# Which queue issues the small transfers of a hybrid decoder layer: SyncE or GpSimd

## The chip, the cores and the metric

The kernel runs on one core of a Trainium2 chip. The metric is the device time of one execution in microseconds (us). The core's engines are TensorE (PE, with PEld for its weight loads), VectorE (DVE), ScalarE (ACT), GpSimd (POOL) and SyncE (SP); SP runs no arithmetic and here only issues transfers (DMAs). Each engine works through its own instructions in order and waits for others by semaphores.

## The reference

One layer of a decoder on 1024 tokens with 1024 features, all in float32. Two mixers read one common input projection:

```python
h = rmsnorm(x, norm1_w); proj = h @ w_in
o_a = gated_delta_rule(q_a, k_a, v_a, g, beta)              # 4 heads of 128, chunked
o_a = rmsnorm(o_a, gdn_norm_w) * silu(z)
o_b = dilated_attention(q_b, k_b, v_b)                      # 8 heads of 64, three (window, dilation) branches
x = x + concat([o_a, o_b]) @ w_out
h = rmsnorm(x, norm2_w)
u = causal_dwconv(h @ w_up, ffn_conv_w)                     # width 3
x = x + (silu(gate) * up) @ w_down
return rmsnorm(x, final_norm_w)
```

In the attention the three branches are merged by their softmax denominators; each output is a sum of values divided by one total denominator per token and head.

## The kernel before

Activations are kept with features on the 128 partitions and tokens along the row. Every large product is made of three TensorE products of split operands (`whi`, `wlo` and so on: a rounded high part and the rest). A weight tile is loaded into `wst` by SP, ScalarE rounds it into `whi`, and VectorE or, for the later dense tiles, GpSimd subtracts to give `wlo`.

A planner (`Weave`, line 49) runs generators for the parts of the layer (dense projections, the four heads' chains, attention, output projection, MLP) and chooses by estimated ready times which of them emits its next instructions. It fixes TensorE's order by a token on each product. The order on the other engines is then made by a scheduler that simulates the program, so that an instruction can be emitted earlier or later than its neighbours in the code. Objects of the class `Engine` hold the planner's costs and the engine that gets the instruction: `ve` and `uv` are VectorE, `ac` and `ua` ScalarE, `po_` GpSimd, `sy` transfers on SP, and `sq` small transfers, on SP too. Nearly all instructions carry line 142 or 144 (the helper in `Engine`), so they are told apart by their tiles.

`sq` is used in four places:

- `finish(h)` (line 926), for heads 2 and 3: the chain's output `vtok`, scaled on GpSimd by `ms`, is transposed in 32x32 blocks by VectorE into `ot`, and eight transfers per head write it to `odram` in runs of 32 numbers (512 runs each).
- `dense()` (line 617): four transfers per head read it back as `og` in 256 runs each. `og` is needed much later, when the gate `z` is multiplied in.
- `rows_out` (line 1052), for each of the attention's groups 0 to 6 (a group is half the tokens of one pair of heads): VectorE transposes the reciprocal denominators `dn` into `dt`, four transfers store it to `ddram`, two load it back as `rT`, each row repeated over 64 partitions.
- `rms2_power` (line 1291), once: the second norm's factors go through `ndram`; their broadcast load back into `rstdB` is issued by `sy`.

```python
    dt = tile_(sp, [P, 32], F32, "dt", "dt", 2)                                   # rows_out
    ve.transpose(dt, dns[g["n"] % 2])
    for b in range(4):
        sq.dma_start(to[:, 32 * b:32 * b + 32], dt[32 * b:32 * b + 8, :])
    rT = g["rT"] = tile_(sp, [P, 512], F32, "rT", "t2", 2)
    for e, er in enumerate(HALVES):
        sq.dma_start(rT[er].rearrange("p (u t) -> p u t", u=4), ...)
```

Attention is a pipeline over pairs of 128-row blocks; two pairs make a group. In each step (`advance`, line 1117) TensorE makes scores, VectorE adds the mask and takes the maximum (`sm`, `mx`), ScalarE exponentiates `sm`, TensorE transposes it, VectorE and ScalarE copy it to `pt` and `pb`, and TensorE multiplies with the values. `give` (line 1101) scales a finished group on VectorE: `oT` = sums times `rT`. Dense products (for `aqkv`, the next heads' queries and keys, drained by VectorE) fill TensorE between the steps. The tiles `ot`, `rT` and `oT` take turns in two buffers (`t2`). After the second norm's statistics, the first channel tile of the MLP is scaled as `xu` by `rstdB`, while VectorE goes on preparing weight blocks (`pair` and others).

Of the kernel before, what the change touches and what calls it, by code (L numbers as in the profile page):

```python
# [147 lines left out]
def hybrid_layer(tc, I, out):  # L148
    nc = tc.nc
    wv = Weave()  # L150
# [4 lines left out]
    ua = Engine(wv, nc.scalar, "scalar", 0.12, 0.00085, first=tc.high_priority)  # L155
    po_ = Engine(wv, nc.gpsimd, "gpsimd", 0.15, 0.0021)
    sy = Engine(wv, nc.sync, "sync", 0.05, 0.00142, 2.2)
    sq = Engine(wv, nc.sync, "small", 0.05, 0.00036, 0.4)
    sa = Engine(wv, nc.scalar, "actq", 0.05, 0.00142, 2.2)
    es = ExitStack()  # L160
    cp = es.enter_context(tc.tile_pool(name="cp", bufs=1))
# [1582 lines left out]
```

## Time and profile before

| | us |
|---|---|
| median of 3 runs | 1196.23 (1195.36 to 1197.35) |
| the profiled execution | 1197.55 |
| its span, first to last instruction | 1195.7 |
| TensorE busy | 1182.3 |
| VectorE / ScalarE / GpSimd busy | 918.3 / 569.5 / 81.5 |

The granted TensorE clock was 0.998 of full speed. Times in views are from the start of the span. SP's issues are shown with the time that the issue takes on SP, not with the transfer's flight. Nearly all transfers are on SP's queue.

### The profile page before, as it was taken

How to read it: one execution, taken by the hardware profiler on the slowest of the kernel's cores; microseconds unless marked ns; L12 is line 12 of the kernel's file. 1: busy time of each engine (PE TensorE's matmuls, PEld its weight loads, DVE VectorE, ACT ScalarE, POOL GpSimd, SP SyncE). 2: the span in 40 equal slices, each digit the busy share in tenths (PEclk: the TensorE clock that was granted, in tenths of full speed). 3: DMA queues.
4: the chain of work that ended last, by engine and by line, in shares of the span. 5: the costliest groups of instructions: out<-in, count | busy, mean ns of one | idle time of the engine just before them, and what ended most of it. 6: DMA issues, size and time to landing. Idle time of an engine off the chain costs nothing.

```text
span 1195.7 us, 18260 instructions
## 1 busy us (share of the span) xinstructions
PE 1182.3 (99%) x6998; PEld 977.3 (82%) x6998; DVE 918.3 (77%) x1473; ACT 569.5 (48%) x1115; POOL 81.5 (7%) x74
## 2 busy tenths in 40 slices
PE   9999999999999999999999999999999999999997
PEld 7888888888777778888888888888888888887886
DVE  7673975666365665777898898989889889998875
ACT  7275345355354533555554444445444453434441
POOL 0212010214211110000000000000000000000000
PEclk9999999999999999999999999999999999999999
DMA  7334234435944214443322313132231397546514
GB/s 244 101 95 150 80 116 127 143 122 172 220 147 129 86 52 135 159 159 106 106 86 73 106 53 106 54 106 81 78 103 56 127 368 284 197 160 211 168 53 141
DMA packets 100023, 157.20 MB, mean 131 GB/s; under 512 B 30400, under 2 KB 51168, under 8 KB 99936
## 3 DMA queue, kind: packets, MB, share of 16 engines
q1 hardware_dynamic: 99072, 155.25, 40.1%
q8 instruction: 55, 0.90, 0.3%
q10 hardware_dynamic: 864, 0.79, 0.2%
q14 instruction: 32, 0.26, 0.1%
HBM read 120.04 MB, written 35.96 MB: 130 GB/s over the span
## 4 chain that ended last, share of the span: by engine, by line
PE 93%; DVE 3%; ACT 2%; issue 1%; DMA 1%; POOLq 0%; POOL 0%; DVEq 0%; SPq 0%; ACTq 0%
PE ps L194 45%; PE pa L194 20%; PE dw L194 15%; PE pc L194 10%; PE ps L198 2%; DVE kT L142 1%; DMA wd<-in_wd 1%; DVE x1h L142 0%; ACT sm L144 0%; DVE pr L142 0%; DMA xt<-in_xT 0%; ACT whi L142 0%; DVE zz L142 0%; DVE wd L142 0%; ACT dec L142 0%
## 5 line engine op out<-in xcount | busy, mean ns | idle before, releaser
L194 PE MATMUL dw<-pr 128*128 128x512 f32 (+1 forms) x984 | 212.0, 377 | 0.3 <-DVE x1h L142 0.2
L194 PEld LDWEIGHTS dw<-pr 128*128 128x128 f32 x984 | 176.6, 188 | 34.7 <-DVE x1h L142 1.2
L194 PE MATMUL ps<-xhi,whi 128*128 128x512 f32 x384 | 157.1, 409 | 0.1
L194 PE MATMUL ps<-xhi,wlo 128*128 128x512 f32 x384 | 150.1, 391 | 0.0
L194 PE MATMUL ps<-xlo,whi 128*128 128x512 f32 x384 | 148.3, 390 | 0.0
L194 PE MATMUL pa<-T,pair 128*128 128x512 f32 x528 | 127.1, 389 | 0.1
L194 PEld LDWEIGHTS pa<-T,pair 128*128 128x128 f32 x528 | 99.0, 188 | 20.9 <-ACT u L142 0.5
L194 PEld LDWEIGHTS ps<-xhi,whi 128*128 128x128 f32 x384 | 72.3, 188 | 19.1 <-issue 5.6
L194 PEld LDWEIGHTS ps<-xhi,wlo 128*128 128x128 f32 x384 | 72.2, 188 | 15.6
L194 PEld LDWEIGHTS ps<-xlo,whi 128*128 128x128 f32 x384 | 72.3, 188 | 12.6
L142 ACT ACTIVATE u<-pa 128x512 f32<-128x512 f32 x44 | 26.3, 598 | 108.7 <-PE pa L194 108.7
L142 DVE SCALAR_TENSOR_TENSOR y<-xu,fcw,y 128x1023 f32<-128x1023 f32 (+1 forms) x44 | 56.4, 1281 | 23.3 <-ACT y L142 23.2
L142 ACT ACTIVATE whi<-wst 128x1024 fp32r<-128x1024 f32 x36 | 38.2, 1065 | 63.6 <-PE ps L194 45.9
L194 PE MATMUL pa<-B,A 128*128 128x512 f32 x264 | 63.4, 389 | 0.0
L194 PE MATMUL pc<-T,S 128*128 128x512 f32 x264 | 63.4, 389 | 0.0
L194 PE MATMUL pa<-T,S 128*128 128x512 f32 x264 | 63.4, 389 | 0.0
L194 PE MATMUL pc<-B,pair 128*128 128x512 f32 x264 | 63.4, 389 | 0.0
L142 ACT ACTIVATE pr<-r 128x1024 fp32r<-128x1024 f32 (+1 forms) x44 | 36.6, 840 | 51.8 <-PE dw L194 29.5
L142 DVE TENSOR_TENSOR wst<-wst 128x512 f32<-128x512 f32 x88 | 60.4, 687 | 0.8
L194 PE MATMUL ps<-B,pair 128*128 128x512 f32 x252 | 60.5, 389 | 0.0
L194 PEld LDWEIGHTS pa<-T,S 128*128 128x128 f32 x264 | 49.6, 188 | 10.3
L194 PEld LDWEIGHTS pc<-B,pair 128*128 128x128 f32 x264 | 49.6, 188 | 10.3
(255 smaller groups left out, 2322.5 us busy)
## 6 DMA issues: line engine op xcount, KB each, us to landing
wst<-in_wu SPq DMA_DIRECT2D x44, 512.0 KB
wd<-in_wd SPq DMA_DIRECT2D x44, 512.0 KB
upark<-y SPq DMA_DIRECT2D x22, 512.0 KB
wst<-in_wi SPq DMA_DIRECT2D x21, 512.0 KB
r<-upark SPq DMA_DIRECT2D x11, 512.0 KB
r<-upark SPq DMA_DIRECT2D x22, 256.0 KB
wa<-in_wd SPq DMA_DIRECT2D x22, 256.0 KB
wst<-in_wv SPq DMA_DIRECT2D x8, 512.0 KB
```

The lines of the kernel that those rows point to most:

```text
L142: return getattr(eng, op)(*a, **kw)
L194: tc.stamp_issue_order_token(nc.tensor.matmul(dst, lhs, rhs, start=start, stop=stop, **kw).ins, TOKEN)
L198: tc.stamp_issue_order_token(nc.tensor.transpose(dst, src, ident if idt is None else idt).ins, TOKEN)
```

## The change

The one object `sq` gets GpSimd in the place of SP. All its transfers (16 `odram`, 8 `og`, 28 `ddram`, 14 `rT`, 4 `ndram`) are issued by GpSimd then; the planner's costs for them stay.

```diff
     po_ = Engine(wv, nc.gpsimd, "gpsimd", 0.15, 0.0021)
     sy = Engine(wv, nc.sync, "sync", 0.05, 0.00142, 2.2)
-    sq = Engine(wv, nc.sync, "small", 0.05, 0.00036, 0.4)
+    sq = Engine(wv, nc.gpsimd, "small", 0.05, 0.00036, 0.4)
     sa = Engine(wv, nc.scalar, "actq", 0.05, 0.00142, 2.2)
```

TensorE's order is the same instruction for instruction. The scheduler places some others anew. GpSimd around the end of the chains and the first groups of attention, before (`vtok` and `ms` are a head's output and its factors, `wlo` a weight split, `pb` a cleared part of an attention tile):

```order
L142 TENSOR_TENSOR wlo<-wst,whi 128x1024
L142 MEMSET pb 32x2x128
L142 TENSOR_TENSOR ms<-ms,mhalf 128x8
L142 TENSOR_TENSOR vtok<-vtok,ms 128x1024
L142 TENSOR_TENSOR wlo<-wst,whi 128x1024 x2
L142 MEMSET pb 32x2x128
```

The same place in the changed kernel:

```order
L142 DMA odram<-ot 32x16x32 x8
L142 MEMSET pb 32x2x128
L142 TENSOR_TENSOR ms<-ms,mhalf 128x8
L142 TENSOR_TENSOR wlo<-wst,whi 128x1024
L142 DMA og<-odram 32x8x128 x4
L142 TENSOR_TENSOR vtok<-vtok,ms 128x1024
L142 DMA odram<-ot 32x16x32 x4
L142 TENSOR_TENSOR wlo<-wst,whi 128x1024
L142 DMA odram<-ot 32x16x32 x4
L142 DMA ddram<-dt 8x32 x4
L142 DMA og<-odram 32x8x128 x4
L142 DMA rT<-ddram 64x4x128 x2
```

Head 2's stores stand ahead of head 3's factors `ms`; head 2's loads `og`, which wait for those stores to land, stand ahead of head 3's scaling `vtok`; and group 0's `ddram` and `rT` stand behind head 3's stores and loads. For group 1 a `wlo` follows between `ddram` and `rT`; the same holds for groups 3 and 6.

VectorE at the start of attention, where head 3's output is transposed into `ot`, before:

```order
L142 TENSOR_SCALAR ms<-ms 128x8
L142 TENSOR_TENSOR aqkv<-ps,rstdB 128x4x32x4
L142 STREAM_TRANSPOSE ot<-vtok 128x128 x8
L142 TENSOR_TENSOR aqkv<-ps,rstdB 128x4x32x4
L144 ISA sm,mx<-ps,mk 128x128
```

And in the changed kernel:

```order
L144 ISA sm,mx<-ps,mk 128x256
L144 ISA mx 128x1
L144 RECIPROCAL dn<-mx 128x2
L142 STREAM_TRANSPOSE ot<-vtok 128x128 x8
L142 TENSOR_TENSOR aqkv<-ps,rstdB 128x4x32x4
L144 RECIPROCAL dn<-mx 128x2
```

The transposes of head 3 have moved behind the four `sm` and the first `dn` of the attention's first pair. They also wait now for head 2's stores, since both use the buffers of `ot`.

VectorE at the end of group 0, where `oT` of group 0 stands, before:

```order
L144 COPY pt<-ps 128x4x64
L144 COPY pb<-ps 128x2x64
L142 TENSOR_TENSOR oT<-ps,rT 128x4x4x32
L144 ISA sm,mx<-ps,mk 128x416
L144 ISA mx 128x1
```

And in the changed kernel:

```order
L144 ISA sm,mx<-ps,mk 128x448
L144 ISA mx 128x1
L144 RECIPROCAL dn<-mx 128x2
L142 TENSOR_TENSOR oT<-ps,rT 128x4x4x32
L144 RECIPROCAL dn<-mx 128x2
L142 STREAM_TRANSPOSE dt<-dn 128x32
L142 TENSOR_TENSOR aqkv<-ps,rstdB 128x4x32x4
```

`oT` of group 0 has moved behind the four `sm` of the next pair and one `dn`; `dt` of group 1 follows it. In groups 1 to 6 `oT` stands where it stood, ahead of the next pair's `sm`. In the first channel tile of the MLP, `xu` has moved behind one `pair` on VectorE.

## The prediction

> **What bounds the kernel now.** The page first: the busy times, then the chain that ended last.
>
> ```profile
> span 1195.7 us, 18260 instructions
> PE 1182.3 (99%) x6998; PEld 977.3 (82%) x6998; DVE 918.3 (77%) x1473; ACT 569.5 (48%) x1115; POOL 81.5 (7%) x74
> PE 93%; DVE 3%; ACT 2%; issue 1%; DMA 1%; POOLq 0%; POOL 0%; DVEq 0%; SPq 0%; ACTq 0%
> ```
>
> TensorE is the bound: 13.4 us of idle in the whole span. The change touches the stretch from about 298 to 428 us (chain outputs, attention) and one place at 566 us. The stage view of TensorE there (columns: length, PE busy, instructions, clock, DMA share, GB/s):
>
> ```profile
> 300.00:320.00 20.00, 20.00 (x97) 1.00 0.95 207
> 320.00:340.00 20.00, 18.74 (x261) 1.00 0.52 150
> ...
> 420.00:440.00 20.00, 19.60 (x270) 1.00 0.18 54
> ```
>
> TensorE idles 1.26 us in the second row and 0.40 us in the third. Nothing here can give back more than about 1.7 us, and every delay that reaches TensorE is lost: its order is fixed and it has no later idle time to catch up in. How near the delays are to it is seen in one softmax step of attention (timelines of VectorE, ScalarE and TensorE):
>
> ```profile
> 353.27 0.46 DVE L144 CUSTOM_DVE_ANT_0 sm<-ps,mk 128x288 f32<-128x288 f32 x1 [0.24 <-PE ps L194]
> 355.89 0.19 ACT L144 ACTIVATION_READ_ACCUMULATOR sm<-sm,mx 128x1 f32 x1
> 356.19 0.96 PE L198 MATMUL ps<-ident,sm 64*128 64x64 f32 x24
> ```
>
> VectorE waits 0.24 us for the scores, ScalarE's last exponential ends at 356.08, and TensorE turns the result at 356.19. What holds VectorE back by more than about 0.3 us stops TensorE.
>
> **What the transfers do on SP.** For each group of scores `dt` (the turned reciprocals) is stored in four pieces, loaded as `rT` in two, and `oT` is scaled with it. Timelines of SP's queue and VectorE, groups 0, 1, 4, 5 and 6 of the seven:
>
> ```profile
> 329.48 1.34 SPq L142 DMA_DIRECT2D ddram<-dt  x4
> 331.70 1.29 SPq L142 DMA_DIRECT2D rT<-ddram  x2
> ```
> ```profile
> 329.24 0.21 DVE L142 STREAM_TRANSPOSE dt<-dn 128x32 f32<-128x32 f32 x1
> 337.96 1.09 DVE L142 TENSOR_TENSOR oT<-ps,rT 128x512 f32<-128x512 f32 x1 [0.88 <-PE ps L194]
> 343.10 0.21 DVE L142 STREAM_TRANSPOSE dt<-dn 128x32 f32<-128x32 f32 x1
> 351.95 1.08 DVE L142 TENSOR_TENSOR oT<-ps,rT 128x512 f32<-128x512 f32 x1 [2.10 <-PE ps L194]
> ...
> 383.42 0.21 DVE L142 STREAM_TRANSPOSE dt<-dn 128x32 f32<-128x32 f32 x1
> 398.99 1.09 DVE L142 TENSOR_TENSOR oT<-ps,rT 128x512 f32<-128x512 f32 x1 [0.88 <-PE ps L194]
> 404.13 0.21 DVE L142 STREAM_TRANSPOSE dt<-dn 128x32 f32<-128x32 f32 x1
> 412.72 1.08 DVE L142 TENSOR_TENSOR oT<-ps,rT 128x512 f32<-128x512 f32 x1 [2.10 <-PE ps L194]
> 417.18 0.21 DVE L142 STREAM_TRANSPOSE dt<-dn 128x32 f32<-128x32 f32 x1
> 427.78 1.08 DVE L142 TENSOR_TENSOR oT<-ps,rT 128x512 f32<-128x512 f32 x1 [0.90 <-PE ps L194]
> ```
>
> From `dt` to `oT` there are 8.7 us in group 0, 8.85 in group 1, 15.6 in group 4, 8.6 in group 5, 10.6 in group 6; groups 2 and 3 repeat 0 and 1. Today's chain: 0.24 us to the first store, 1.34 for four, 0.88 until they have landed, 1.29 for two loads (to 332.99), and then their flight. The stage view shows when that ends:
>
> ```profile
> 334.00:335.00 1.00, 1.00 (x7) 0.81 (x5) 1.00 (x3) 1.00 (x5) 0.00 (x0) 1.00 0.43 120
> 335.00:336.00 1.00, 1.00 (x24) 0.69 (x24) 0.50 (x4) 0.43 (x3) 0.00 (x0) 1.00 0.01 2
> ```
>
> The DMA engines fall from a share of 0.43 to 0.01 at 335.0: 2.0 us of flight, 5.8 us of chain in all, and 3.0 us of slack in group 0.
>
> **The price of an issue on GpSimd.** The trace has no DMA issued by GpSimd, so it is bounded. Below by what the same transfer takes on SP (tile views: min/median/max ns); above by GpSimd's own small and whole-tile operations (mean ns):
>
> ```profile
> L142 SPq DMA_DIRECT2D ddram<-dt x28: 269/288/458, 329.5 to 418.4; - x28
> L142 SPq DMA_DIRECT2D rT<-ddram x14: 579/613/629, 331.7 to 420.3; - x14
> L142 SPq DMA_DIRECT2D odram<-ot x16: 303/502/1822, 298.2 to 316.4; - x16
> L142 SPq DMA_DIRECT2D og<-odram x8: 551/605/955, 305.7 to 320.6; - x8
> L142 POOL TENSOR_TENSOR ms<-ms,mhalf 128x8 f32<-128x8 f32 x4 | 6.5, 1637 | 12.3 <-DVE ms L142 12.2
> L142 POOL TENSOR_TENSOR wlo<-wst,whi 128x1024 fp32r<-128x1024 f32 x12 | 28.5, 2376 | 91.9 <-ACT whi L142 86.5 <-PE ps L198 5.5
> ```
>
> For the tiny `ddram` store the ends are 0.29 and 1.64 us; for the others, in 256 or 512 pieces, SP's median and 2.38. Neither end is nearer in kind, so I take the middles: `ddram` 0.96, `rT` and `og` 1.49, `odram` 1.44 us. I leave the flights as measured; a longer flight counts like a dearer issue.
>
> [...]
>
> **Groups 1 to 6.** The chain becomes 0.24 + 4 x 0.96 + 0.88 + 2 x 1.49 + 2.0 = 9.9 us. In groups 1, 3 and 6 a weight split `wlo` now stands on GpSimd between the stores and the loads; its 2.38 us cover the 0.88 of landing, and the chain is 11.5 us. Late by: group 1 2.6, group 2 1.2, group 3 2.6, group 4 nothing, group 5 1.4, group 6 0.9; together 8.7 us. `oT` stands in front of the next scores' `sm` on VectorE, so this passes to TensorE less the 0.24 us seen above.
>
> **Group 0.** Here GpSimd's queue holds the chain outputs of heads 2 and 3 as well. These rows time it (VectorE's timeline, GpSimd's timeline, SP's):
>
> ```profile
> 310.17 1.67 DVE L142 STREAM_TRANSPOSE ot<-vtok 128x128 f32<-128x128 f32 x8 [0.61 <-POOL vtok L142]
> 321.62 0.17 DVE L144 RECIPROCAL dn<-mx 128x2 f32<-128x2 f32 x1 [1.37 <-ACT sm L144]
> 341.62 0.16 DVE L144 RECIPROCAL dn<-mx 128x2 f32<-128x2 f32 x1
> ```
> ```profile
> 323.10 2.37 POOL L142 TENSOR_TENSOR wlo<-wst,whi 128x1024 fp32r<-128x1024 f32 x1 [10.61 <-ACT whi L142]
> ```
> ```profile
> 298.17 5.08 SPq L142 DMA_DIRECT2D odram<-ot  x8
> ```
>
> In the new order the transposes of head 3 stand behind the first `dn` of attention, so their first half is ready at 321.8 + 0.8 = 322.6. From there GpSimd runs 4 `odram` (5.8), `wlo` (2.4), 4 `odram` (5.8), 4 `ddram` (3.8), 4 `og` (6.0), 2 `rT` (3.0): 349.4, and 351.4 with the flight. `oT` of group 0 has been moved behind the `dn` that ended at 341.8. Late by 9.6 us, and `dt` of group 1 and the copies `pt` that TensorE needs stand behind it. Head 2's eight stores, from 298.2, with what follows them there (`ms`, `wlo`, four `og` and `vtok`, the last at no more than the price of a `wlo`: 24 us in all) end by 322, about when head 3's transposes can start anyway.
>
> The weight splits themselves stay hidden: the one at 323.10 would end at 330.8, and it serves the dense tile that TensorE begins after `aqkv` is drained behind the `dt` of 343.10. Without that cover its 5 us would be lost too.
>
> **Second norm.** Four stores of `ndram` go to GpSimd, the broadcast load `rstdB` stays on SP (SP's queue, VectorE, TensorE):
>
> ```profile
> 566.24 1.30 SPq L142 DMA_DIRECT2D ndram<-dt  x4
> 572.12 1.23 DVE L142 TENSOR_TENSOR xu<-xu,rstdB 128x1024 f32<-128x1024 f32 x1 [1.07 <-DMA rstdB<-ndram]
> 573.26 1.22 DVE L142 TENSOR_TENSOR pair<-wst,pair 128x1024 fp32r<-128x1024 f32 x1
> ...
> 586.30 2.88 PE L194 MATMUL pa<-T,pair 128*128 128x512 f32 x12
> ```
>
> The stores end 3.84 - 1.30 = 2.5 us later and so does `xu`. The new order puts `pair` ahead of it, and TensorE uses that `pair` 12 us later: hidden, nothing in the sum; bare, 2.5 us.
>
> **SP's queue** loses 70 issues. They stood among loads that nobody on TensorE waits for, so this gives nothing beyond the 1.7 us above, and I count nothing.
>
> **The sum.** 9.6 + 8.7 = 18.3 us, less 0.24 for each of five late steps (1.2): 17.1. The profiled execution took 1197.55 us (span 1195.7), 1.3 us over the median of the runs, 1196.23. So 1214.7 for it, and 1213.3 against the median.
>
> **The rivals.** [...] 0.11.
>
> *The chain outputs clog GpSimd*: at the upper prices head 2's eight stores take 19 us and its `og` 9.5, the scaling `vtok` of head 3 ends at 333 instead of 322, group 0's `rT` lands at 378, 36 us late, and the chains of 14.4 and 15.9 us add 31: 1263. It decides from about 2 us for an `odram`. For it: 512 pieces each. Against: SP needs only 0.5 us. 0.14.
>
> *Not slower but faster*: the loads that stood behind waiting small stores on SP come sooner and the 1.7 us vanish: 1194.5. That is under 0.2%, about what a measurement of this kernel can tell from no change; for more, idle time would have to go elsewhere, and none hangs on SP. 0.03.
>
> **How the numbers follow.** The forecast, stalls at `oT` between 3 and 49 us, has 0.72, its middle 1213. Faster by over 0.2% 0.03, within it 0.11, slower 0.72 + 0.14 = 0.86. The range runs from 1195.5 (the no-change case) to 1245 (well towards the clogged case, which is left out with its 0.14).
>
> **What would show it.** Right: VectorE waits for `rT` before `oT` in groups 0, 1, 2, 3 and 5, most in group 0; TensorE idles about 17 us more between 340 and 430 and nowhere else; GpSimd's issues last 0.9 to 1.5 us. Wrong: issues of 0.6 us or less and an unchanged 300 to 440; or `ot` late on VectorE before 322; or new idle time after 570.

## The result, and the profile after

Over 16 runs each, the changed kernel took 1199.49 us (1197.42 to 1201.0) and the kernel before 1197.10 us (1195.36 to 1200.66): a ratio of 1.0019, with a 95% interval of 1.0011 to 1.0027. It is slower by 2.4 us, or 0.2%, where 17.1 us had been forecast. The profiled execution took 1199.3 us.

The page after, in the lines shown of before:

```profile
span 1197.4 us, 18271 instructions
...
PE 1182.7 (99%) x6998; PEld 977.5 (82%) x6998; DVE 918.3 (77%) x1473; ACT 569.0 (48%) x1115; POOL 122.3 (10%) x144
...
PE 92%; DVE 2%; ACT 2%; DMA 2%; issue 1%; POOL 0%; POOLq 0%; DVEq 0%; SPq 0%; ACTq 0%
```

GpSimd is busy 41 us longer, with 70 more instructions, the 70 transfers. The stage view of TensorE, one row of before, then after:

```profile
340.00:360.00 20.00, 20.00 (x270) 1.00 0.60 172
```
```profile
320.00:340.00 20.00, 18.74 (x261) 1.00 0.52 144
340.00:360.00 20.00, 19.16 (x235) 1.00 0.63 175
...
380.00:400.00 20.00, 20.00 (x235) 1.00 0.68 173
...
420.00:440.00 20.00, 19.00 (x239) 1.00 0.18 54
```

Before, 340 to 360 had no idle time and 420 to 440 had 0.40 us; now there are 0.84 and 1.00. TensorE's order is the same in both kernels, so each product's start can be set against its start before. This lag grows by 1.55 us in the transposes at 356 (the products ahead of them start 0.26 us earlier than before, those behind them 1.29 us later) and by 0.68 us at 424, and otherwise only by what two executions of one kernel differ by; the two places make 2.23 us, beside the 2.4 us between the medians. At the first, TensorE's timeline has

```profile
356.42 2.02 PE L198 MATMUL ps<-ident,sm 64*128 64x64 f32 x24 [0.43 <-ACT sm L144]
```

where before the same 24 transposes took 0.96 us and waited for nothing.

What an issue takes on GpSimd (tile views: min/median/max ns):

```profile
L142 POOL DMA_DIRECT2D ddram<-dt x28: 497/511/540, 330.3 to 420.5; - x28
L142 POOL DMA_DIRECT2D rT<-ddram x14: 632/637/665, 337.4 to 424.1; - x14
L142 POOL DMA_DIRECT2D odram<-ot x16: 648/650/912, 298.9 to 329.7; - x16
L142 POOL DMA_DIRECT2D og<-odram x8: 582/582/635, 311.5 to 336.8; - x8
```

0.51 to 0.65 us, and nearly the same for 8 runs as for 512. The prediction had taken 0.96 to 1.49.

VectorE's timeline, groups 0 to 3:

```profile
341.63 1.07 DVE L142 TENSOR_TENSOR oT<-ps,rT 128x512 f32<-128x512 f32 x1
...
342.87 0.21 DVE L142 STREAM_TRANSPOSE dt<-dn 128x32 f32<-128x32 f32 x1
...
354.27 1.08 DVE L142 TENSOR_TENSOR oT<-ps,rT 128x512 f32<-128x512 f32 x1 [4.68 <-DMA rT<-ddram]
...
358.21 0.21 DVE L142 STREAM_TRANSPOSE dt<-dn 128x32 f32<-128x32 f32 x1
...
366.37 1.09 DVE L142 TENSOR_TENSOR oT<-ps,rT 128x512 f32<-128x512 f32 x1 [0.88 <-PE ps L194]
...
371.50 0.21 DVE L142 STREAM_TRANSPOSE dt<-dn 128x32 f32<-128x32 f32 x1
...
383.82 1.06 DVE L142 TENSOR_TENSOR oT<-ps,rT 128x512 f32<-128x512 f32 x1 [5.59 <-DMA rT<-ddram]
```

Group 0's `oT` waits for nothing. From `dt` to `oT` group 1 takes 11.4 us (8.85 before) and group 3 12.3 (8.8 before), and there `oT` waits for `rT`. Group 2 takes 8.2 and waits for TensorE, as it did before; groups 4, 5 and 6 wait for TensorE too. GpSimd's timeline from head 3's stores to group 1:

```profile
322.81 2.59 POOL L142 DMA_DIRECT2D odram<-ot  x4 [7.06 <-DVE ot L142]
...
330.31 2.03 POOL L142 DMA_DIRECT2D ddram<-dt  x4
335.07 2.35 POOL L142 DMA_DIRECT2D og<-odram  x4 [2.72 <-DMA odram<-ot]
337.40 1.27 POOL L142 DMA_DIRECT2D rT<-ddram  x2
...
343.37 2.04 POOL L142 DMA_DIRECT2D ddram<-dt  x4 [4.35 <-DVE dt L142]
345.47 2.39 POOL L142 TENSOR_TENSOR wlo<-wst,whi 128x1024 fp32r<-128x1024 f32 x1
348.44 1.29 POOL L142 DMA_DIRECT2D rT<-ddram  x2 [0.58 <-DMA ddram<-dt]
```

Group 0's queue is the one foreseen, in its order and from the moment foreseen (322.6), but it is through at 338.7 instead of 349.4. In group 1 the issue of the last store ends at 345.41 and that of the first load starts at 348.44, when the store has landed: 3.0 us for 4 KB, against 0.9 on SP. The split `wlo` between them ends at 347.86, so it alone would have held the load for 2.4 of the 3.0 us. SP's queue in group 1, first in the kernel before, then in the changed one:

```profile
344.67 0.34 SPq L142 DMA_DIRECT2D apark<-aqkv  x1
345.57 1.25 SPq L142 DMA_DIRECT2D rT<-ddram  x2
346.91 0.56 SPq L142 DMA_DIRECT2D wst<-in_wi  x1
347.56 0.38 SPq L142 DMA_DIRECT2D kT<-apark  x1
```
```profile
344.28 0.32 SPq L142 DMA_DIRECT2D apark<-aqkv  x1
...
347.61 0.32 SPq L142 DMA_DIRECT2D kT<-apark  x1
348.03 0.37 SPq L142 DMA_DIRECT2D wst<-in_wi  x1
```

SP's queue before had the 512 KB store `apark` behind `ddram`, and the 512 KB loads `wst` and `kT` behind `rT`. Now `apark` goes out at 344.28 while GpSimd is still issuing `ddram`, and both loads go out ahead of `rT`. The trace's records of single packets show what comes of it (first packet to last):

```
group 1     before                    after
ddram       344.08 to 345.17          344.47 to 347.10
apark       345.50 to 346.96          345.09 to 347.07
rT          346.95 to 348.99          351.45 to 353.08
wst, kT     348.32 to 352.07          348.56 to 351.78
```

The small transfers now lie among or behind the large ones. In groups 2 and 5 of the same trace, with no load ahead, the last packet of `rT` came 1.9 us after GpSimd's issue had ended; in group 1 it came 3.4 us after. Group 1's delay is made of the dearer stores (0.75 us), of the split and of this.

The second place, 424, is an operation of VectorE beside one of GpSimd; timelines of the two, before and then in the changed kernel:

```profile
417.94 2.38 POOL L142 TENSOR_TENSOR wlo<-wst,whi 128x1024 fp32r<-128x1024 f32 x1 [5.45 <-PE ps L198]
418.78 2.62 DVE L142 SCALAR_TENSOR_TENSOR zz<-zz,xr 128x1024 f32<-128x1024 f32 x1
421.43 1.23 DVE L142 TENSOR_TENSOR og<-og,zz 128x1024 f32<-128x1024 f32 x1
```

```profile
421.06 2.47 POOL L142 TENSOR_TENSOR wlo<-wst,whi 128x1024 fp32r<-128x1024 f32 x1
421.32 3.29 DVE L142 TENSOR_TENSOR og<-og,zz 128x1024 f32<-128x1024 f32 x1
```

`og` took 1.23 us before. Now the subtraction `wlo` stands behind the four `ddram` (2.03 us), starts 0.26 us ahead of `og`, and `og` takes 3.29, to 1.1 us after the subtraction's end. Before, the subtraction ran from 417.94 beside `zz`, which took 2.62 us where it takes 1.23 now, and less of that reached TensorE.

The second norm, last (VectorE's timeline):

```profile
575.78 1.23 DVE L142 TENSOR_TENSOR xu<-xu,rstdB 128x1024 f32<-128x1024 f32 x1 [0.35 <-DMA rstdB<-ndram]
```

`xu` waits 0.35 us for its factors where it waited 1.07 before, since it now stands later, and TensorE loses nothing there.

### The profile page after: what moved, and what is told of

Its sections match the earlier page's. It is cut to its first block, busy times and chain, and to the rows that moved or that the text cites. A ratio compares the mean times of both kernels' runs of the same rounds, so it can differ in the third digit from the quotient of the medians.

```text
span 1197.4 us, 18271 instructions
## 1 busy us (share of the span) xinstructions
PE 1182.7 (99%) x6998; PEld 977.5 (82%) x6998; DVE 918.3 (77%) x1473; ACT 569.0 (48%) x1115; POOL 122.3 (10%) x144
## 4 chain that ended last, share of the span: by engine, by line
PE 92%; DVE 2%; ACT 2%; DMA 2%; issue 1%; POOL 0%; POOLq 0%; DVEq 0%; SPq 0%; ACTq 0%
PE ps L194 44%; PE pa L194 20%; PE dw L194 17%; PE pc L194 10%; PE ps L198 2%; DMA r<-upark 1%; ACT sm L144 1%; DVE kT L142 1%; DMA rT<-ddram 0%; DMA xt<-in_xT 0%; DVE sm L144 0%; DVE og L142 0%; DMA ddram<-dt 0%; DVE x1h L142 0%; ACT whi L142 0%
## 5 line engine op out<-in xcount | busy, mean ns | idle before, releaser
L142 POOL TENSOR_TENSOR rs<-rs,mhalf 128x2 f32<-128x2 f32 (+2 forms) x4 | 4.8, 1204 | 735.6 <-DVE rs L144 735.6
```

The lines of the kernel that those rows point to most:

```text
L142: return getattr(eng, op)(*a, **kw)
```

## Experiments

Three theories. *Place*: a small transfer is late because it has lost its place ahead of SP's large ones. *Price*: it is late because GpSimd's issues take time, and the prediction's steps are right with another price. *Collision*: the loss at 424 is `og` beside the subtraction. The losses quoted below as "TensorE's lag" are read like the 1.55 and 0.68 above: starts of the same products against the kernel before. In the diffs `gq_` is the object on GpSimd while `sq` is back on SP. Each run has its ratio to the kernel before on the same chip.

**Which half of the change.** Only the attention's transfers on GpSimd:

```diff
-    sq = Engine(wv, nc.gpsimd, "small", ...)
+    sq = Engine(wv, nc.sync, "small", ...); gq_ = Engine(wv, nc.gpsimd, "small", ...)
-                    sq.dma_start(to[...], dt[32 * b:32 * b + 8, :])     # ddram; rT likewise
+                    gq_.dma_start(to[...], dt[32 * b:32 * b + 8, :])
```

> Only the reciprocals (ddram and rT) are issued by GpSimd; chain outputs and the second norm's factors stay on SP. Both theories put the loss here: F (the flight of rT, now behind the loads that SP issues earlier) and P (GpSimd's queue: dearer issues and a weight split between ddram and rT). Expected 1.5 to 3 us over before; oT of group 1 waits for rT and TensorE falls behind by about 1.4 us at the transposes that follow; another 0.7 us at about 424 us, where the weight split holds og on VectorE. If it is within 1 us of before, the loss belongs to the chain outputs or the norm.

1201.90 us, 1.0041 (1.0027 to 1.0055), more than the whole change. In group 1 `oT` waits for `rT` until 355.91. TensorE's stages there (columns as above):

```profile
357.00:358.00 1.00, 0.00 (x0) 1.00 1.26 137
...
360.00:361.00 1.00, 1.00 (x14) 0.50 0.38 136
...
363.00:364.00 1.00, 1.00 (x37) 0.95 0.01 0
```

After the gap, of 1.51 us, the granted clock is 0.50 for 3.4 us; as an estimate, half of that stretch, 1.7 us, is the most that it costs. The lag from this one wait is 4.2 us. The prediction had no term for that.

The other half, chain outputs and the norm's factors (`odram`, `og`, `ndram`) on GpSimd, the attention's on SP, by the same kind of edit:

> Only the chain outputs (odram, og) and the second norm's factors (ndram) are issued by GpSimd; the reciprocals stay on SP. F and P both expect the time of before within 1 us: og is needed over 100 us later, the weight splits have 15 us of cover, and the later xu is hidden behind the weight blocks. If it is slower by 1.5 us or more, neither holds.

1199.36 us, 1.0017 (1.0009 to 1.0026), not the no-change expected. Of its trace's lag 1.5 us is a stretch at half clock from 323.2 to 326.6, behind the 1.1 us gap that every one of these kernels has at 322; of the kernels below, one with all small transfers on SP shows it too, so it is not put down to the edit. Another 1.65 us are at 344 to 348. Timelines of SP and VectorE in group 0:

```profile
330.17 1.55 SPq L142 DMA_DIRECT2D ddram<-dt  x4
...
335.64 1.28 SPq L142 DMA_DIRECT2D rT<-ddram  x2
...
341.17 1.07 DVE L142 TENSOR_TENSOR oT<-ps,rT 128x512 f32<-128x512 f32 x1 [3.38 <-DMA rT<-ddram]
```

Here `ddram` lands 3.9 us after its last issue, and `rT` is late, though both are on SP: head 3's stores and `og` from GpSimd now lie beside them, where SP had done with them at 316 and 321. The two halves cost 4.1 and 1.7 thousandths, the whole 1.9: they do not add up; each half is scheduled anew and has its own order.

**Are SP's large loads to blame?** The queries, keys and values of later head pairs are not loaded again (the first pair's data stay in use, so the attention's output is that of other data; by the DMA records 6.3 MB less are moved, not 4.5), with the small transfers on SP and then on GpSimd:

```diff
+    kept = []
+
     def att_load(pi):
+        if kept:
+            return kept[0]
+        kept.append(att_load_all(pi))
+        return kept[0]
+
+    def att_load_all(pi):
```

> The kernel before, without the loads of the attention's queries, keys and values for the pairs of heads 1 to 3: the tiles of the first pair are used again, so these outputs are left wrong and 4.5 MB less are moved. It is the base for the next run. F and P: TensorE-bound as before, 1194 to 1197 us, oT never waits for rT.

> The changed kernel (all small transfers on GpSimd, GpSimd's order the same), also without the loads of queries, keys and values for pairs 1 to 3. F: with those loads gone rT of groups 1 and 3 flies in about 2 to 3 us instead of 4.5 and 6.0, oT of both no longer waits for it by more than 0.5 us, TensorE loses nothing there, and at most the 0.7 us at about 424 us stay over the run without loads on SP. P: the weight split still stands between ddram and rT, so oT of groups 1 and 3 still waits 2 us or more beyond TensorE's own release and the loss of 2 us over the run without loads on SP stays.

1196.52 us, 0.9992 (0.9983 to 1.0001), and 1198.85 us, 1.0014 (1.0003 to 1.0024). In the trace of the second, `rT` has one load in front of it (`wst`, packets 348.29 to 350.46) instead of two; its packets run from 349.73 to 351.69, and `oT` waits only for TensorE:

```profile
352.43 1.07 DVE L142 TENSOR_TENSOR oT<-ps,rT 128x512 f32<-128x512 f32 x1 [3.43 <-PE ps L194]
```

Against its twin TensorE loses 0.28 us at 356 instead of 1.55, and the same 0.66 at 424. That speaks for place in group 1, but the trace is of the fastest of the kernel's 11 executions, 1196.75 us: the medians of the two kernels differ by 2.3 us, no less than with the loads in place, and the traces' lags by 0.9. This is taken up below.

**At the prediction's own prices.** Every attention and chain transfer cut in two, so that two issues cost about what one had been taken for (the line shown, and three more of the kind); then only `ddram`:

```diff
-                    sq.dma_start(to[:, 32 * b:32 * b + 32], dt[32 * b:32 * b + 8, :])
+                    for i in (0, 16): sq.dma_start(to[:, 32 * b + i:32 * b + i + 16], dt[32 * b:32 * b + 8, i:i + 16])
```

> The changed kernel with each of the attention's small transfers cut in two, all on GpSimd: 8 stores of reciprocals and 4 reads of them per group, 16 chain stores and 8 chain reads per head. At the 0.51 to 0.65 us an issue that the changed kernel showed, a pair of halves costs GpSimd 1.0 to 1.3 us, close to the 0.96 to 1.49 us that the prediction had taken for one. Theory price (the prediction's steps were right and only the price was wrong): every group gets 2.0 us more of ddram and 1.3 us more of rT, the chain outputs 5 us more; oT waits for rT in most groups, TensorE loses 10 to 17 us against the kernel before, 1207 to 1214 us. Rival slack (VectorE's lateness does not reach TensorE whatever its size, as the 3 us of group 3 did not): at most 2 to 5 us over the changed kernel, 1201 to 1204 us.

> The changed kernel with only the stores of the reciprocals cut in two, 8 for 4 in each group, on GpSimd. Eight at 0.51 us are 4.1 us, near the 3.84 us (4 x 0.96) that the prediction had taken for four. Theory price: 2.05 us more in each of seven groups, of which group 1, where TensorE already waits, gives all, groups 2, 5 and 6, which have about 1 to 2 us left, give up to 1 us each, and groups 0 and 3 little: 1202 to 1206 us. Rival slack: group 1 alone, 1201.5 us. Either way a longer gap in TensorE near 356 us, of about 2.5 us, and if a gap of this length halves the clock for 3.4 us as in the kernel with only the reciprocals moved, 1.7 us on top.

1202.61 us, 1.0041 (1.0028 to 1.0055), and 1203.16 us, 1.0040 (1.0027 to 1.0053). The pieces cost what was meant (`rT`'s halves 0.60 us):

```profile
L142 POOL DMA_DIRECT2D ddram<-dt x56: 499/511/563, 329.2 to 428.5; - x56
```

So at about the forecast's prices the loss is some 5 us and not 17. It is no clean test of the price, for the scheduler, with more issues to place, has moved `oT` of several groups further back: in the first kernel group 0's stands behind `dt` of group 2, waits for nothing and ends at 358.3. What the two runs do show is that dearer issues need not become loss in full.

**The collision.** The last two weight splits on VectorE, in the changed kernel and in the kernel before:

```diff
-                nxt.append(weight(None, st=raw.pop(), spare=i >= 17))
+                nxt.append(weight(None, st=raw.pop(), spare=17 <= i < 27))
```

> The changed kernel with the last two of the weight splits that GpSimd computes given to VectorE, so that no GpSimd subtraction stands beside VectorE's og near 421 us. Theory collision (the 0.68 us that TensorE loses near 424 us comes from og taking 3.29 us instead of about 1.2 us while GpSimd's subtraction runs): og takes 1.2 to 1.4 us, the loss near 424 us goes, 0.5 to 0.9 us less than the changed kernel, 1198.6 us, unless the two splits cost VectorE as much elsewhere. Rival (og late for another reason, its read of rT or the landing of its inputs): og keeps 3 us, time as the changed kernel, 1199.5 us.

> The kernel before (all small transfers on SP) with the last two of GpSimd's weight splits given to VectorE, so that VectorE's zz near 419 us does not stand beside GpSimd's subtraction. Theory collision: zz takes 1.2 us instead of 2.62, the 0.40 us that TensorE idles between 420 and 440 us goes, 0.2 to 0.5 us less than the kernel before, about what can't be told from no change. Rival: the two splits take VectorE 2.4 us where it is needed, and the time is the same or up to 0.5 us more.

1198.17 us, 1.0002 (0.9991 to 1.0012), and 1196.84 us, 1.0000 (0.9992 to 1.0009). In the first, VectorE's timeline and TensorE's stage:

```profile
423.13 1.23 DVE L142 TENSOR_TENSOR og<-og,zz 128x1024 f32<-128x1024 f32 x1
```
```profile
420.00:440.00 20.00, 20.00 (x249) 1.00 0.17 54
```

`og` is back at 1.23 us, and TensorE idles nothing where it idled 1.00. Set against each other, the traces of the two kernels part by 1.7 us at 357 and by 0.9 at 373, and by nothing at 424. Collision stands. The edit also saved the kernel before about 1 us between 419 and 443 in its trace (0.40 of it idle time), so not all that it gave the changed kernel is the collision's; the time of 1196.84 us cannot be told from that of the kernel before.

**Store or read?** One hop back on SP, the rest as changed: first `rT`, then `ddram`.

> The changed kernel with the reads of the reciprocals (rT) back in SP's queue; their stores, the chain outputs and the norm's factors stay on GpSimd. In group 1 SP's order is again kT, rT, weight load, four vn, two vc. Theory queue (rT's flight of 4.5 us in group 1 comes from the six loads that SP starts at once, where before they stood behind rT): rT lands in 2 to 3 us, TensorE's loss near 356 us falls from 1.39 us to 0 to 0.5 us, 1198.0 us. Rival landing (the late part is the store from GpSimd, 3.0 us to land in group 1): rT is issued as late as in the changed kernel and TensorE still loses 1 us or more there, 1199.5 us.

> The changed kernel with only the stores of the reciprocals (ddram) back in SP's queue; their reads (rT), the chain outputs and the norm's factors stay on GpSimd. Theory order (in group 1 GpSimd's stores and reads lose their place ahead of SP's three 512 KB transfers, so each waits for the DMA engines to work these off): on SP the stores are ahead of the transfer behind them again and land in 0.9 to 1.2 us instead of 3.0, rT goes out by 347 us ahead of the load kT or beside it and lands by 351 to 352 us, oT waits for TensorE only, and the loss of 1.4 us near 356 us goes to 0 to 0.4; the 0.7 us near 424 us stays: 1198.2 us. Rival price (a read issued by GpSimd is late whatever stands ahead of it): oT of group 1 still waits for rT until 353.5 us or later, TensorE loses 1 us or more near 356 us, 1199.5 us.

1201.60 us, 1.0032 (1.0020 to 1.0044), and 1199.90 us, 1.0021 (1.0011 to 1.0032). Neither took the loss away. (The trace with `ddram` on SP is of the slowest of its ten executions.) Timelines of SP, GpSimd and VectorE in group 1, `rT` on SP, then `ddram` on SP:

```profile
349.68 0.32 SPq L142 DMA_DIRECT2D kT<-apark  x1
350.23 1.24 SPq L142 DMA_DIRECT2D rT<-ddram  x2
...
356.73 1.07 DVE L142 TENSOR_TENSOR oT<-ps,rT 128x512 f32<-128x512 f32 x1 [4.52 <-DMA rT<-ddram]
```
```profile
345.96 2.35 POOL L142 TENSOR_TENSOR wlo<-wst,whi 128x1024 fp32r<-128x1024 f32 x1 [5.76 <-ACT whi L142]
...
348.35 0.36 SPq L142 DMA_DIRECT2D wst<-in_wi  x1
...
348.80 1.24 POOL L142 DMA_DIRECT2D rT<-ddram  x2 [0.48 <-DVE mx L144]
...
356.72 1.07 DVE L142 TENSOR_TENSOR oT<-ps,rT 128x512 f32<-128x512 f32 x1 [5.23 <-DMA rT<-ddram]
```

As I had worded it, that the queue of `rT` decides, the theory fell: on SP too `rT` flies 5.3 us (351.47 to 356.73). In this kernel's order `kT` stands ahead of it, and GpSimd's stores landed late, with packets to 349.35. With the store on SP it was the split `wlo` that held `rT` on GpSimd until `wst` had gone. What the runs share is the place. Issued ahead of the loads on SP, the last packet of `rT` came 2.2 us after its issue had ended in the kernel before, and 1.9 in the run with the chain outputs on GpSimd, though that issue started as late as 348.75. Issued by GpSimd with a load ahead or beside it, the last packet came 3.0 to 5.6 us after (eight traces), and on SP behind `kT` it was late as well. This is a pattern over kernels with different orders; no run takes the place away and leaves the rest.

So both holds were taken away at once, `ddram` on SP and that one split on VectorE, with the split's move alone in the kernel before as its price:

```diff
-                nxt.append(weight(None, st=raw.pop(), spare=i >= 17))
+                nxt.append(weight(None, st=raw.pop(), spare=i >= 17 and i != 24))
```

> The changed kernel with the stores of the reciprocals (ddram) in SP's queue, and with GpSimd's weight split of group 1, which in the run with ddram on SP held rT back until 348.8 us, given to VectorE; rT stays on GpSimd. Now nothing stands before rT: it goes out when ddram has landed, 2.5 us after dt, near 346.5 us, ahead of SP's loads wst and kT. Theory place (a read of reciprocals takes 2 to 2.5 us if it goes out before SP's 512 KB loads and 4.5 to 6.7 us behind one of them, whichever engine issues it): rT's flight in group 1 is at most 3 us, oT waits for TensorE only, and the loss near 356 us goes from 2.0 us to 0.3 us or less; VectorE's split may cost up to 1 us near 351 us, as in the kernel before with the same edit. Rival GpSimd (its reads are slow whatever stands ahead): flight of 4.5 us or more, oT waits for rT and TensorE loses 1 us or more near 356 us.

> Beside the run with ddram on SP and one split moved: the kernel before with that same split of group 1 given to VectorE, all small transfers on SP. It prices the split's move alone, by which the other run is to be read: VectorE is held up 1.2 us in the middle of group 1, TensorE loses 0 to 1 us near 351 us, none near 356 us; 1197 to 1198 us. By theory place and by rival GpSimd alike.

1200.97 us, 1.0028 (1.0015 to 1.0041), and 1198.39 us, 1.0010 (1.0001 to 1.0018). The first is inconclusive: `rT` went out at 348.46 and not at 346.5, behind `wst` again; its packets ended at 352.69, and `oT` did wait for TensorE only, but TensorE was some 4.5 us late itself by then, in part from a gap of 1.09 us and half clock behind it. The second gives a price by the way: 1.2 us more on VectorE in group 1 cost TensorE 1.1 us.

**Is anything left?** Both named causes away at once, no reloads and no last splits, with the small transfers on GpSimd and on SP; and the changed kernel again.

> The changed kernel with both named causes taken away: the queries, keys and values of later head pairs are not loaded again (the first pair's stay in use, so the attention's output is that of other data), and GpSimd's last two weight splits are VectorE's. Theory two causes: TensorE loses nothing near 356 nor near 424 us, and the time is within 0.5 us of its twin with the small transfers on SP, 1196 to 1197 us. Rival third cause (GpSimd's transfers cost somewhere that one trace does not show, or make landings vary from run to run): 1 us or more above the twin.

> The twin: the kernel before, all small transfers on SP, with the same two things taken away (no reloads of queries, keys and values, so other data; the last two of GpSimd's splits on VectorE). By either theory 1196 to 1197 us: the run without reloads alone took 0.9992 of the kernel before, the run with the two splits moved 1.0000.

> The changed kernel once more, for its time and trace on the same chip as the two runs beside it. By either theory 1.001 to 1.003 of the kernel before, TensorE idle 0.8 us between 340 and 360 us and 1.0 us between 420 and 440 us; by the theory that a gap of TensorE of 1.1 us or more can halve its clock for 3.4 us, perhaps such a dip after the gap at 322 us, which every kernel here has.

1196.90 us, 0.9995 (0.9985 to 1.0006); 1196.85 us, 0.9993 (0.9984 to 1.0002); 1199.71 us, 1.0021 (1.0011 to 1.0030). The medians of the twins agree to 0.05 us, uncertain by somewhat over 1 us, and the changed kernel beside them stands 2.8 us above: with both edits no loss is left that the times could tell. How the two causes share it the times do not show. With only the reloads away the medians of the two kernels still stood 2.3 us apart, with only the two splits moved 1.3 us (by the ratios 2.6 and 0.2 us), where the traces of the changed kernel and the kernel before put 1.55 us at 356 and 0.68 at 424. So the medians give more to the splits and less to the loads than the traces do, and each of these differences is uncertain by 1 to 1.6 us. Nor does the first edit clear the queue: `apark`, `wst` and the split in group 1 stay. The execution profiled of the kernel on GpSimd, 1197.89 us and above its median, still shows `oT` of group 1 waiting for `rT` until 353.53, and falls behind its twin by 0.86 us at 356 and by 0.91 at 374.

The second trace of the changed kernel has the same two losses (1.41 us at 356, 0.67 at 424) and a third place, group 2:

```profile
364.29 1.26 POOL L142 DMA_DIRECT2D rT<-ddram  x2 [3.85 <-DMA ddram<-dt]
368.21 1.06 DVE L142 TENSOR_TENSOR oT<-ps,rT 128x512 f32<-128x512 f32 x1 [3.02 <-DMA rT<-ddram]
```

In the first trace the same wait for the store took 1.6 us, and `oT` did not wait for `rT`; here 1.31 us of lag follow. The packets show the difference. Each time the store's data are through 0.6 us after the last issue, and 96 packets of 4 bytes go with them. Here the last two of these come at 362.68, when a 16 KB packet of an instruction queue (361.73 to 362.69) has ended. In the first trace that packet (362.20 to 363.16) came after all 96. The same two late packets, at the end of the same 16 KB packet, stand in two more traces, of the changed kernel without the last two splits and without both causes, whose group 2 waited for `rT` too (2.7 and 2.6 us). That the one held up the others is read from the times alone. It is a third place of loss beside the two causes, and no run took it away.

## Why the prediction was wrong

*TensorE is the bound, and nothing can be won.* Right: what the changed kernel's trace loses shows as idle TensorE or as lag between 340 and 430, and no kernel that did all the work with transfers on GpSimd was faster than the kernel before.

*The price of an issue.* This step failed. The prediction bounded it by SP's 0.29 to 0.61 us and GpSimd's 1.64 and 2.38 us for arithmetic, called neither end nearer in kind, and took middles of 0.96 to 1.49. Measured: 0.51 to 0.65, near the lower end. The upper rows were of arithmetic on elements, while the issues took nearly the same for 8 runs as for 512 (0.51 us against 0.65); SP's rows were the same operation and were the nearer ones. The prediction had named issues of 0.6 us or less, with the stretch from 300 to 440 unchanged, as the sign that it is wrong; the first half of that came near, the second did not.

*Group 0, 9.6 us late.* Fell with the price. The queue from 322.8 took 15.9 us to the end of `rT`'s issue, where 26.8 had been counted (4 + 4 `odram`, `wlo`, 4 `ddram`, 4 `og`, 2 `rT`), though it held one wait not counted, 2.72 us for `odram` to land. `rT` was there for the `oT` that the new order had put at 341.63. This term alone was more than half of the sum.

*Groups 1 to 6, 8.7 us.* Group 1 was forecast 2.6 us late and `dt` to `oT` is 2.55 longer; group 3 forecast 2.6, measured 3.5. That the sizes are near is in part luck. From `dt` to the last packet of `rT` group 1's chain grew from 5.9 to 10.2 us, by 4.3, where 5.7 had been counted. The dearer issues of `ddram` are 0.75 of it, a later first issue 0.26, and the time from the last store's issue to the first load's 2.1. Of these 2.1 us the split, which the prediction had right, explains 1.5; the last 0.6 are slower landing. Then come 1.2 us of the flight of `rT`, where 1.7 had been counted for dearer issues of it and nothing for the flight. So the chain was taken 1.4 us too long. The slack was taken 1.2 us too long as well, which nearly evens it out: the prediction ended the flight at the last packet, and wherever `oT` waited for `rT` it started only 0.7 to 1.4 us after that packet. The step that failed here is the sentence that leaves the flights as measured: 0.88 and 2.0 us had been read from group 0 on SP, where `rT` had no large transfer in front of it. Groups 2, 5 and 6 were forecast 1.2, 1.4 and 0.9 us late and were on time in the first trace; group 2 was late in the second.

*What passes to TensorE.* Forecast: all of it, less 0.24 us. Group 1 passed 1.55 of 2.55 us and group 3 nothing of 3.5: TensorE is busy 20.00 of 20.00 us from 380 to 400, with dense products to work on. VectorE's 0.24 us of slack was read in group 1 and carried over to the others.

*The weight splits stay hidden.* Wrong in one place. The split near 421 cost TensorE 0.68 us, not by being late but by standing beside `og`. The rows of before had shown it: `zz` at 2.62 us against 1.23 for the operation beside it.

*The second norm is hidden.* Right. *SP's relief gives nothing.* Right as to a gain, and incomplete: SP, no longer held by waits on small stores, sends its loads earlier relative to the small transfers (in group 1 `kT` at 347.61 and `wst` at 348.03, ahead of `rT` at 348.44, where both had stood behind it). By the trace that has a part in the larger of the two losses; the times of the kernels do not show how large a part.

*The rivals.* The no-change case, which had 0.11, came nearest: the changed kernel is 0.19% slower. Its issues are not far from SP's (0.51 to 0.65 us against 0.29 to 0.61), and yet time was lost: in group 1 between the last store's issue and the first load's (3.0 us against 0.9) and in the flight of `rT` (3.4 us against 2.2 to the last packet), and near 424 in `og` beside a neighbour on another engine (3.29 us against 1.23). By the packets it took 1.09 us from the first `ddram` issue to its first packet in groups 2 to 5, and 0.75 on SP. These 0.34 us alone, against the 3.0 us of slack in group 0, would by an estimate have moved nothing, and that alone is not what happened.

## What to carry over

One queue is also an order: when small latency-critical transfers leave a queue, look at what large transfer stood behind them there, since it may now go ahead: here, with 1 MB ahead, the first packet of `rT` came 3.0 us after its issue began, against 1.4 in the kernel before and in groups 2 and 5 of the changed kernel, with no load ahead. Price an operation on another engine by the same operation's rows first, and take a flight from a row only together with what lay in front of it. An instruction that moves by a few microseconds on an idle engine may land beside one that then takes longer: here `wlo`, begun at 421.06 and not at 417.94, beside `og`, which took 3.29 us and not 1.23. The row of before that pointed to it was `zz`, at 2.62 us beside `wlo`.

## What the runs showed of the hardware

- Behind some gaps of TensorE more was lost than the gap. Its granted clock fell to 0.50 for about 3.4 us after gaps of 1.51 us (only the attention's transfers on GpSimd), of 1.81 us (the kernel with all transfers cut in two) and of 1.09 us (`ddram` on SP and one split on VectorE); behind the 1.1 us gap near 322 that all 17 profiled executions have, it fell in 4 of the 17. After five other gaps of 1.0 to 1.1 us (four near 65, one near 977) it did not fall, and after gaps below 1 us it never did (the kernel's last 10 us, where TensorE runs out of work, left out). Where it can be told apart, the lag grew by about 1.5 us each time.
- Between the last packet of the store `ddram` and the issue of `rT` lay 0.3 to 0.8 us in the kernel before, with both on SP, and 1.0 to 1.3 us in groups 1, 2, 4 and 5 of the changed kernel. Either can be longer: 1.6 us in group 0 of the run with the chain outputs alone on GpSimd (both on SP), and 3.2 us in group 2 of the changed kernel's second trace.
- GpSimd sent the same `rT` as 64 packets of 4 KB, where SP's had been 512 packets of 512 bytes.
